# Loading w_down by whole rows and computing its two column halves together, in a two-layer mixer and mixture-of-experts kernel

## The chip, the cores and the metric

The kernel runs on one core of a Trainium2 chip. The metric is the device time of one execution in microseconds (us), the median of three runs. The core has five engines with an instruction stream each: PE (TensorE, matmuls and transposes), DVE (VectorE), ACT (ScalarE), POOL (GpSimd) and SP (SyncE, which here only issues DMAs). Each takes its instructions strictly in order, and a wait on a semaphore holds back all that is queued behind it on that engine.

## What is computed

x is 512 tokens by 1024, everything is float32. There are two layers, each a token mixer beside a cross-attention to 256 memory tokens, an output projection, a layer norm, sixteen experts of which each token uses two, and another layer norm:

```python
for i in range(DEPTH):                                  # 2 layers
    if i % 2 == 0:
        z = x @ w_in_a                                  # u | v | q
        uv = gelu(z[..., :1024]);  u, v = split(uv)
        tok = u * (W_s @ layer_norm(v, sgu_ln_g, sgu_ln_b) + sgu_b)
    else:
        z = x @ w_in_b;  tok = short_conv_mixer(...)    # uses conv_w
    xa = memory_cross_attention(q, mem, w_kv[i])
    x = layer_norm(ALPHA * x + concat(tok, xa) @ w_out[i], ln1)
    for e in range(16):                                 # chosen tokens only
        h = silu(xt @ w_gate[i, e]) * (xt @ w_up[i, e])
        f += combine[:, e] * (h @ w_down[i, e])
    x = layer_norm(ALPHA * x + f, ln2)
```

w_gate and w_up of an expert are 1024 by 512, w_down is 512 by 1024: 2 MB each, so 6 MB for an expert and 192 MB for both layers.

## The kernel before, in words

**Precision.** Every float32 product is made of three matmuls on rounded operands (mm3, L172 to L176): high by high, high by low, low by high. Each weight block is therefore split after it has landed: ACT copies it to a rounded `high` (L144), DVE (now and then POOL) subtracts to get `low` (L145). A matmul of line L174 or L176 needs `high`, one of L175 needs `low`.

**Storage.** SBUF is cut into 24 pages of 8 KB per partition. Every raw weight load, split and activation takes a page and gives it back (`page`, `drop`).

**The stream of weights** (class `Stream`, object W). `todo` is a list of loads of 1 MB, issued by SP in order as pages come free; `keep` is the number of pages that must be left free when a load is issued, `ahead` the number of splits made in advance, `flight` the number of loads under way. w_gate and w_up are read in two halves over k (4096 contiguous bytes at a time), w_down in two halves over its columns (2048 bytes at a time). An expert's loads in order are gate 0, up 0, gate 1, up 1, then the two halves of w_down of the expert before.

**An expert.** The up to 128 tokens that chose it are gathered (POOL, `xg`), transposed on PE (`xt`, L648) and copied into `xgt` by ACT in two halves. `xgt` exists once: the copy of its first half for the next expert has to wait until PE has used this expert's first halves of w_gate and w_up, and so on for the second. PE computes `ga` and `ua`, ACT takes silu of `ga` (L664), DVE multiplies (L665), PE transposes the product (`htr`), ACT and DVE split it into `ht` (L179, L180; it also exists once, so its new content waits for the last matmul that reads the old). `down` computes one column half after the other into accumulators `ya`, and ACT moves each out, scaled by the gate value, when it is complete (L686). The rows are then scattered to memory by POOL (L635). w_down of expert e-1 is computed behind gate and up of expert e; only the last expert stays on the chip and is added by a selection matmul (`ra`, L745 to L747), together with x, which SP reads back from memory (L728) after the last scatter.

**Order.** A scheduler decides the order of instructions on each engine when the program is built; it is static. So an edit to the loads also reorders ACT, DVE and PE.

**Mixer of layer 0** (L943 to L1000). After the keys and values, x is transposed and multiplied by w_in_a in three parts: q, then v (`vp`, gelu, statistics), then u (L979, gelu). `norm` (L426 to L437) normalises v: L434 subtracts the mean and multiplies by the gain, L437 multiplies by the reciprocal deviation and adds the bias; gain and bias are in page `sgln`, loaded on ACT's queue. `attend` transposes the attention weights (PE `pt`, split by ACT L179 and DVE L180), multiplies by the values (`xa`), and the results are split into `ch` and `cl`. `mx` is the product with W_s; the output projection is `oa`.

## Time and profile before

| | us |
|---|---|
| median of three runs | 1069.66 (1065.61 to 1069.82) |
| the profiled execution | 1064.45 |
| its span, first to last instruction | 1062.8 |
| outside the span | 1.65 |
| mixer of layer 0 | 0 to 217 |
| experts of layer 0 | 217 to 531 |
| layer norm, mixer of layer 1 | 531 to 725 |
| experts of layer 1 | 725 to 1040 |
| layer norm, output | 1040 to 1063 |

PE is the busiest engine; what is to be read is where it waits, for whom, and what that engine was doing. A row of the timeline gives the start, the duration, the engine, the line, the operation and, in brackets, how long the engine stood still before it and what it waited for. A row of the windows gives, for each engine, busy time in a stretch, then the granted PE clock as a share of full speed, the busy share of the 16 DMA engines, and their rate.

### The profile page before, as it was taken

What the parts mean: (1) busy time and instruction counts of PE and PEld (TensorE: products, weight loads), DVE (VectorE), ACT (ScalarE), POOL (GpSimd) and SP (SyncE); (2) the same over time, 40 slices, a digit from 0 to 9 for tenths busy, and PEclk for the clock granted to TensorE, in tenths of its full rate; (3) what the DMA queues carried; (4) which work ended last, traced back from release to release, by engine and by line L of the source; (5) the groups of instructions that cost most, each with busy time, mean ns of one, the idle gap of its engine ahead of it and who ended that gap; (6) DMA issues with size and microseconds to landing.
All of it is one profiled execution on the core that took longest, in us unless ns stands there. A gap on an engine that the chain in (4) does not pass through costs nothing.

```text
span 1062.8 us, 12859 instructions
## 1 busy us (share of the span) xinstructions
PE 989.5 (93%) x4815; PEld 809.4 (76%) x4816; DVE 779.6 (73%) x880; ACT 630.6 (59%) x684; POOL 177.1 (17%) x115
## 2 busy tenths in 40 slices
PE   8999999789999988999999999987899999988995
PEld 6788889668888876777678887875788888866863
DVE  4648657869898677878794656575799898768875
ACT  4536524458888667668553524234778887667762
POOL 0000014312212202001100000223053212220113
PEclk9999999979999999999999999987899999999998
DMA  9713449459999999979671424491699999999833
GB/s 327 269 41 119 156 162 319 160 195 360 358 370 371 367 349 365 336 274 321 200 280 40 159 79 152 146 401 45 210 355 362 372 361 360 347 359 336 282 68 154
DMA packets 102220, 273.31 MB, mean 257 GB/s; under 512 B 10442, under 2 KB 10966, under 8 KB 102152
## 3 DMA queue, kind: packets, MB, share of 16 engines
q1 hardware_dynamic: 89480, 242.84, 62.9%
q0 software_dynamic: 11808, 26.97, 9.2%
q10 hardware_dynamic: 864, 2.62, 0.7%
q8 instruction: 39, 0.64, 0.2%
q14 instruction: 29, 0.24, 0.1%
HBM read 262.22 MB, written 26.21 MB: 271 GB/s over the span
## 4 chain that ended last, share of the span: by engine, by line
PE 61%; DVE 8%; ACT 4%; DMA 4%; issue 2%; DVEq 0%; ACTq 0%; POOLq 0%; SPq 0%
PE ua L175 5%; PE ua L176 5%; PE ya L175 5%; PE ya L174 5%; PE ua L174 5%; PE ya L176 5%; PE ga L175 5%; PE ga L174 4%; PE ga L176 4%; DVE low L145 4%; ACT high L144 3%; PE xt L648 2%; PE za L176 2%; PE za L174 2%; PE za L175 2%; DMA raw<-in_w_up_dram 2%
## 5 line engine op out<-in xcount | busy, mean ns | idle before, releaser
L145 DVE TENSOR_TENSOR low<-raw,high 128x2048 fp32r<-128x2048 f32 x189 | 428.7, 2288 | 78.8 <-ACT high L144 73.0
L144 ACT ACTIVATE high<-raw 128x2048 fp32r<-128x2048 f32 x189 | 357.9, 1914 | 54.5 <-PE ga L175 20.1
L175 PE MATMUL ua<-low,xgt 128*128 128x512 f32 x248 | 98.6, 397 | 16.7 <-DVE low L145 16.6
L144 ACT ACTIVATE split<-raw 128x1024 fp32r<-128x1024 f32 x66 | 68.5, 1058 | 76.7 <-PE za L176 26.1
L174 PE MATMUL ya<-high,ht 128*128 128x512 f32 x256 | 103.9, 407 | 2.5 <-ACT high L144 2.5
L176 PE MATMUL ya<-high,ht 128*128 128x512 f32 x256 | 101.5, 398 | 2.5 <-DVE ht L180 2.5
L175 PE MATMUL ya<-low,ht 128*128 128x512 f32 x256 | 102.6, 401 | 0.7 <-DVE low L145 0.7
L174 PE MATMUL ga<-high,xgt 128*128 128x512 f32 x248 | 98.9, 399 | 3.0 <-ACT high L144 3.0
L175 PE MATMUL ga<-low,xgt 128*128 128x512 f32 x248 | 98.7, 398 | 2.1 <-DVE low L145 1.9
L174 PE MATMUL ua<-high,xgt 128*128 128x512 f32 x248 | 98.1, 395 | 0.2
L176 PE MATMUL ga<-high,xgt 128*128 128x512 f32 x248 | 97.6, 393 | 0.0
L176 PE MATMUL ua<-high,xgt 128*128 128x512 f32 x248 | 97.0, 391 | 0.0
L145 DVE TENSOR_TENSOR split<-raw,split 128x1024 fp32r<-128x1024 f32 x57 | 68.6, 1220 | 38.5 <-ACT split L144 37.8
L639 POOL DMA_INDIRECT xg<-x1d,idxs x32 | 50.3, 1572 | 248.7 <-PE xt L648 238.6
L175 PEld LDWEIGHTS ua<-low,xgt 128*128 128x128 f32 x248 | 46.6, 188 | 30.8 <-DVE low L145 21.6
L145 POOL TENSOR_TENSOR split<-raw,split 128x1024 fp32r<-128x1024 f32 x9 | 21.5, 2390 | 283.2 <-DVE sto L446 146.9
L174 PE MATMUL za<-xh,split 128*128 128x512 f32 x160 | 61.7, 392 | 2.0 <-ACT xh L179 2.0
L635 POOL DMA_INDIRECT rd<-h,idxs x16 | 41.4, 2589 | 127.0 <-ACT h L686 126.4
L175 PE MATMUL za<-xl,split 128*128 128x512 f32 x160 | 62.5, 391 | 0.0
L176 PE MATMUL za<-xh,split 128*128 128x512 f32 x160 | 61.5, 390 | 0.0
L174 PEld LDWEIGHTS ya<-high,ht 128*128 128x128 f32 x256 | 48.8, 191 | 14.3 <-ACT high L144 3.0
L176 PEld LDWEIGHTS ya<-high,ht 128*128 128x128 f32 x256 | 48.4, 189 | 14.6 <-DVE ht L180 3.4
(250 smaller groups left out, 1893.9 us busy)
## 6 DMA issues: line engine op xcount, KB each, us to landing
raw<-in_w_gate_dram SPq DMA_DIRECT2D x64, 1024.0 KB, 10.3
raw<-in_w_up_dram SPq DMA_DIRECT2D x64, 1024.0 KB, 10.1
raw<-in_w_down_dram SPq DMA_DIRECT2D x64, 1024.0 KB, 10.5
raw<-in_w_kv_dram SPq DMA_DIRECT2D x8, 1024.0 KB, 7.3
raw<-in_w_out_dram SPq DMA_DIRECT2D x8, 1024.0 KB, 5.1
raw<-in_w_in_b_dram SPq DMA_DIRECT2D x8, 1024.0 KB, 10.7
raw<-in_w_in_a_dram SPq DMA_DIRECT2D x6, 1024.0 KB, 5.5
x1d<-x POOLq DMA_DIRECT2D x8, 512.0 KB, 5.8
```

The lines of the kernel that those rows point to most:

```text
L144: act.activation(high, src, AF.Copy)
L145: (pool_e if self.on_pool(self.count) else vec).tensor_tensor(low, src, high, op=OP.subtract)
L174: pe.matmul(o, a[0], b[0], start=start, stop=False)
L175: pe.matmul(o, a[0], b[1], start=False, stop=False)
L176: return pe.matmul(o, a[1], b[0], start=False, stop=stop)
L635: added[e] = pool_e.indirect_dma_start(out=rd[i], out_offset=bass.IndirectOffsetOnAxis(ap=tabs[e][0], axis=0), in_=ys[e % 2], in_offset=No ...
L639: pool_e.indirect_dma_start(out=xg[:, e % 2], out_offset=None, in_=x1d[i], in_offset=bass.IndirectOffsetOnAxis(ap=tabs[e][0], axis=0), bou ...
L648: pe.transpose(t[:, k, :], xg[:, e % 2, k0:k0 + 2 * P - 1:2], ident)
```

## The change

- **w_down** of experts 0 to 14 is read by `rows`: a load is two k blocks of 128 rows by all 1024 columns, 4096 contiguous bytes a row. `down` takes the four splits one after the other and multiplies each with both column halves into two accumulators; both are moved out when the last block is done. The last expert keeps the old form.
- **Loads come in units of two**: both halves of a matrix are issued together when two pages are free beyond `keep`, so the loads of an expert are now gate 0, gate 1, up 0, up 1, then w_down. The order in which they are split (`plan`) is given apart from that. The `keep` numbers are raised by one or two. There is code for 2 MB pages, but their number N_DOUBLES is 0.
- **Small operands of mixer 0**: conv_w, sgu_w and sgu_b are loaded after the attention scores instead of at the start, and `sgln` after the u projection. The `norm` of v itself stands at the same place in the code, behind the u projection.

```diff
+        def rows(self, w):
+            ap = lambda k, n: bass.AP(tensor=w.tensor, offset=w.offset + k * D, ap=[[D, P], [P * D, n], [1, D]])
+            return self.add([ap(0, 2), ap(256, 2)], ap(0, 4))
...
+        def fetch(self, single=False):
+            u = self.todo.pop(0)
...
+                for src in u.parts:
+                    t = page("raw", [P, 4, 512])
+                    self.load(t, src)
+                    u.raw.append(t)
...
+            return len(free_pages) >= len(u.parts) + self.keep + max(0, self.ahead - len(self.ready))
...
         def down(e, evict):
+            if e < last:
+                a = [acc("ya") for _ in range(2)]
+                for k in range(4):
+                    g = W.next()
+                    for n in range(2):
+                        mm3(a[n], (ht[:, 0, k, :], ht[:, 1, k, :]), (g[:, 0, n, :], g[:, 1, n, :]), k == 0, k == 3)
+                    W.done(g)
+                for n in range(2):
+                    evict(n, a[n])
+                return
...
         for e in range(E):
-            gu(e, 0)
+            g, u = W.pairs(w_gate[i, e]), W.pairs(w_up[i, e])
+            d = W.rows(w_down[i, e - 1]) if e else None
+            W.use((g, 0), (u, 0))
             if e == E - 1:
-                dn(e - 1)
-            gu(e, 1)
+                W.use((d, 0), (d, 1))
+            W.use((g, 1), (u, 1))
...
-    sg = page("sgln", [P, 2, MW])
-    bcast_rows(sg[:, 0], sgu_ln_g[0])
-    bcast_rows(sg[:, 1], sgu_ln_b[0])
...
     drop(*xh, *xl)
-    W.keep = 5
+    W.keep = 6
+    sg = page("sgln", [P, 2, MW])
+    bcast_rows(sg[:, 0], sgu_ln_g[0])
+    bcast_rows(sg[:, 1], sgu_ln_b[0])
     for c in range(NC):
         norm(vp[:, c, :], sts[:, c, :], sg[:, 0], sg[:, 1], MW)
```

What this does to the order of instructions is shown at three places. The first is DVE in the mixer of layer 0, around the norm of v (L434 and L437 before, L470 and L473 now). Before:

```order
L434 SCALAR_TENSOR_TENSOR v_856<-v_856,mv,sgln_456 128x512
L437 SCALAR_TENSOR_TENSOR v_856<-v_856,rstd,sgln_456 128x512 x2
L431 TENSOR_SCALAR ve<-mv 128x1
L434 SCALAR_TENSOR_TENSOR v_856<-v_856,mv,sgln_456 128x512
L436 RECIPROCAL rstd<-sd 128x1
L437 SCALAR_TENSOR_TENSOR v_856<-v_856,rstd,sgln_456 128x512
L145 TENSOR_TENSOR split_948<-raw_582,split_948 128x1024
L436 RECIPROCAL rstd<-sd 128x1
L437 SCALAR_TENSOR_TENSOR v_856<-v_856,rstd,sgln_456 128x512
L180 TENSOR_TENSOR pt_1029<-pt,pt_1029 128x512 x2
```

Now, on the same engine:

```order
L229 TENSOR_TENSOR pt_1031<-pt,pt_1031 128x512 x2
L470 SCALAR_TENSOR_TENSOR v_853<-v_853,mv,sgln_984 128x512 x2
L473 SCALAR_TENSOR_TENSOR v_853<-v_853,rstd,sgln_984 128x512
L465 BN_AGGR mv<-vst 128x2
L229 TENSOR_TENSOR cl_1029<-xa,ch_1027 128x256
L473 SCALAR_TENSOR_TENSOR v_853<-v_853,rstd,sgln_984 128x512
L465 BN_AGGR mv<-vst 128x2
L229 TENSOR_TENSOR pt_1083<-pt,pt_1083 128x512
...
L473 SCALAR_TENSOR_TENSOR v_853<-v_853,rstd,sgln_984 128x512 x2
L229 TENSOR_TENSOR pt_1057<-pt,pt_1057 128x512 x2
```

The eight operations of the norm stood ahead of the first `pt` split; they now stand among the `pt` splits. On ACT, the two loads of `sgln` now follow the last gelu of u:

```order
L1025 ACTIVATE u_979<-za 128x512
L301 DMA sgln_984<-in_sgu_ln_g_dram 128x512
L301 DMA sgln_984<-in_sgu_ln_b_dram 128x512
L228 ACTIVATE ch_1027<-xa 128x256
L228 ACTIVATE pt_1083<-pt 128x512
L228 ACTIVATE ch_1028<-xa 128x256
L469 ACT_TABLE_LOAD
L469 ACTIVATE sd<-ve 128x1
```

The second place is ACT in layer 1, from the end of expert 10 to expert 11 (raw_7239, 7277 and raw_7276, 7278 are w_down of expert 9, raw_7297 and raw_7326 the first half of w_gate of expert 11; L664 and L700 are silu, L686 and L732 move `ya` out). Before:

```order
L144 ACTIVATE high_7485<-raw_7239 128x2048
L664 ACTIVATE h_5891<-ga 128x512
L144 ACTIVATE high_7503<-raw_7277 128x2048
L179 ACTIVATE xgt_5892<-xt 128x512
L144 ACTIVATE high_7521<-raw_7297 128x2048
L686 ACTIVATE y_170<-ya,gates 128x512
L179 ACTIVATE ht<-htr 128x512
L686 ACTIVATE y_170<-ya,gates 128x512
L144 ACTIVATE high_7559<-raw_7328 128x2048
```

Now:

```order
L700 ACTIVATE h_5887<-ga 128x512
L228 ACTIVATE xgt_5888<-xt 128x512
L179 ACTIVATE high_7485<-raw_7276 128x2048
L228 ACTIVATE xgt_5888<-xt 128x512
L179 ACTIVATE high_7501<-raw_7278 128x2048
L179 ACTIVATE high_7521<-raw_7326 128x2048
L732 ACTIVATE y_167<-ya,gates 128x512
L228 ACTIVATE ht<-htr 128x512
L732 ACTIVATE y_167<-ya,gates 128x512
L179 ACTIVATE high_7578<-raw_7328 128x2048
```

Both splits of w_down of expert 9 now stand behind a copy of `xgt`, the first one too. The block behind the evictions (raw_7328) was the first half of w_up and is the second half of w_gate now.

The third place is the last expert of layer 1 on ACT. raw_7934 and 7952 (before) and raw_8004 and 8006 (now) are w_down of expert 14, raw_7987 and raw_8007 (before) the second halves of w_gate and w_up of expert 15, raw_8038 and 8056 w_down of expert 15; the rows `h<-ya,gates` move expert 14's result out for its scatter. Before:

```order
L144 ACTIVATE high_8137<-raw_7934 128x2048
L144 ACTIVATE high_8166<-raw_7952 128x2048
L144 ACTIVATE high_8182<-raw_7987 128x2048
L144 ACTIVATE high_8199<-raw_8007 128x2048
L686 ACTIVATE h_5891<-ya,gates 128x512 x2
L144 ACTIVATE high_8217<-raw_8038 128x2048
L664 ACTIVATE h_5891<-ga 128x512
L144 ACTIVATE high_8237<-raw_8056 128x2048
```

Now:

```order
L700 ACTIVATE h_5887<-ga 128x512
L179 ACTIVATE high_8136<-raw_8004 128x2048
L179 ACTIVATE high_8166<-raw_8006 128x2048
L179 ACTIVATE high_8216<-raw_8038 128x2048
L179 ACTIVATE high_8237<-raw_8056 128x2048
L732 ACTIVATE h_5887<-ya,gates 128x512
L228 ACTIVATE ht<-htr 128x512
L732 ACTIVATE h_5887<-ya,gates 128x512
```

Expert 14's result is moved out behind all splits and the silu of the last expert, where it stood ahead of them. PE has the same order: it computes w_down of expert 14 after the whole of gate and up of expert 15, and used to compute it between their halves.

## Rows read from the trace of the kernel before

**Rows 1.** The page: busy time by engine; DMA share in 40 slices.

```profile
PE 989.5 (93%) x4815; PEld 809.4 (76%) x4816; DVE 779.6 (73%) x880; ACT 630.6 (59%) x684; POOL 177.1 (17%) x115
...
DMA  9713449459999999979671424491699999999833
```

**Rows 2.** The page: DMA issues of one matrix: KB each, median us to landing.

```profile
PE ua L175 5%; PE ua L176 5%; PE ya L175 5%; PE ya L174 5%; PE ua L174 5%; PE ya L176 5%; PE ga L175 5%; PE ga L174 4%; PE ga L176 4%; DVE low L145 4%; ACT high L144 3%; PE xt L648 2%; PE za L176 2%; PE za L174 2%; PE za L175 2%; DMA raw<-in_w_up_dram 2%
```

**Rows 3.** Busy time by stretch: us, PE, PEld, DVE, ACT, POOL, PEclk, DMA share, GB/s.

```profile
298.00:316.00 18.00, 18.00 (x86) 14.95 (x85) 16.11 (x11) 14.60 (x12) 3.96 (x2) 1.00 1.03 377
414.00:432.00 18.00, 15.94 (x73) 12.32 (x73) 14.21 (x9) 13.12 (x11) 2.63 (x2) 1.00 1.01 349
```

**Rows 4.** DMA queue in 18:36, then 414:432: packets, MB, share; then load issue, split.

```profile
q1 hardware_dynamic: 3225, 6.38, 97.0%
...
q1 hardware_dynamic: 1949, 5.55, 83.1%
...
387.14 0.37 SPq L123 DMA_DIRECT2D raw<-in_w_up_dram  x1
...
421.17 5.52 ACT L144 ACTIVATE high<-raw 128x2048 fp32r<-128x2048 f32 x3
```

**Rows 5.** Mixer 0, timeline of DVE, ACT, PE; then DMA issues: KB, us to landing.

```profile
92.93 0.74 DVE L434 SCALAR_TENSOR_TENSOR v<-v,mv,sgln 128x512 f32<-128x512 f32 x1
...
119.19 0.69 DVE L180 TENSOR_TENSOR pt<-pt,pt 128x512 fp32r<-128x512 f32 x1
119.89 0.42 DVE L180 TENSOR_TENSOR cl<-xa,ch 128x256 fp32r<-128x256 f32 x1
...
115.43 0.60 ACT L979 ACTIVATE u<-za 128x512 f32<-128x512 f32 x1
...
126.18 0.47 PE L174 MATMUL oa<-split,ch 128*128 128x512 f32 x1
...
sgln<-in_sgu_ln_g_dram ACTq DMA_DIRECT2D x1, 256.0 KB, 6.5
...
out_dram<-x SPq DMA_DIRECT2D x1, 256.0 KB, 2.0
```

**Rows 6.** Busy time by stretch, as Rows 3, at the start of layer 1's experts.

```profile
740.00:745.50 5.50, 3.27 (x15) 2.28 (x13) 3.92 (x4) 5.24 (x5) 1.29 (x1) 1.00 0.12 31
745.50:752.00 6.50, 5.76 (x17) 4.66 (x18) 5.78 (x5) 3.46 (x4) 0.00 (x0) 0.50 0.00 0
```

**Rows 7.** Timeline of ACT, DVE and PE at experts 10 and 11 of layer 0.

```profile
420.60 0.68 ACT L686 ACTIVATE y<-ya,gates 128x512 f32<-128x512 f32 x1
...
433.58 0.60 ACT L179 ACTIVATE xgt<-xt 128x512 fp32r<-128x512 f32 x1 [1.89 <-PE ua L175]
...
423.12 6.70 DVE L145 TENSOR_TENSOR low<-raw,high 128x2048 fp32r<-128x2048 f32 x3 [1.69 <-ACT high L144]
...
425.46 0.50 PE L175 MATMUL ua<-low,xgt 128*128 128x512 f32 x1 [1.83 <-DVE low L145]
```

**Rows 8.** Timeline of ACT and PE at the start of layer 1's experts.

```profile
742.50 1.28 ACT L664 ACT_TABLE_LOAD   x1
...
746.24 0.80 PE L174 MATMUL ga<-high,xgt 128*128 128x512 f32 x1 [2.98 <-ACT high L144]
```

**Rows 9.** The end: timeline of ACT, POOL, PE; then DMA issues, us to landing.

```profile
1025.27 0.69 ACT L686 ACTIVATE h<-ya,gates 128x512 f32<-128x512 f32 x1 [1.88 <-PE ya L176]
...
1026.23 1.88 POOL L635 DMA_INDIRECT rd<-h,idxs  x1 [11.97 <-ACT h L686]
...
1039.33 0.40 PE L176 MATMUL ya<-high,ht 128*128 128x512 f32 x1
1039.57 1.02 PE L745 MATMUL ra<-x,ident 128*128 128x512 f32 x2
...
rd<-h,idxs POOLq DMA_INDIRECT x1, 6.6
...
x<-rd SPq DMA_DIRECT2D x1, 512.0 KB, 5.6
```

More of the change, by code (lines that the diff above doesn't have):

```diff
@@ L62, in trunk @@
     uid = [0]
+    free_doubles = list(range(N_DOUBLES))
     def page(name, shape, dtype=FT):
@@ L128, in fetch @@
                                   reason="few loads in flight")
-            self.raw.append([t, 0])
+        def fetch(self, single=False):
+            self.sent += 1
+            u = self.todo.pop(0)
+            if u.whole is not None and free_doubles and not single:
+                u.at, t = double()
+                self.load(t, u.whole)
+                u.raw = [t[:, 0:4], t[:, 4:8]]
+            else:
+                for src in u.parts:
+                    t = page("raw", [P, 4, 512])
+                    self.load(t, src)
+                    u.raw.append(t)
+            u.left = len(u.parts)
         def split(self):
-            t, h = self.raw[0]
+            u, i = self.plan[0]
+            t, h = u.raw[i], self.half
             if self.whole and not h:
@@ L146, in split, with room @@
             self.count += 1
-            if self.raw[0][1] == 2:
-                self.raw.pop(0)
-                drop(t)
+            if self.half == 2:
+                self.half = 0
+                self.plan.pop(0)
+                u.left -= 1
+                if u.at is None:
+                    drop(t)
+                elif not u.left:
+                    free_doubles.append(u.at)
+        def room(self):
+            if not self.todo or len(self.todo) <= self.stop:
+                return False
+            u = self.todo[0]
+            if u.whole is not None and free_doubles:
+                return True
+            return len(free_pages) >= len(u.parts) + self.keep + max(0, self.ahead - len(self.ready))
         def pump(self):
             while True:
-                size = 2 if self.whole and self.raw and not self.raw[0][1] else 1
-                if not self.hold and len(self.ready) + size <= self.ahead and self.raw and len(free_pages) >= size:
+                size = 2 if self.whole and not self.half else 1
+                if (not self.hold and len(self.ready) + size <= self.ahead and self.plan and self.plan[0][0].raw
+                        and len(free_pages) >= size):
                     self.split()
-                elif len(self.todo) > self.stop and len(free_pages) > self.keep + max(0, self.ahead - len(self.ready)):
+                elif self.room():
                     self.fetch()
@@ L936, in trunk @@
     stop += len(W.todo) + W.sent
-    W.keep = 8
+    W.keep = 10
     W.after = last_mem.ins
@@ L948, in trunk @@
             keep_warm(4)
[L949 to L951 removed]
+    W.keep = 6
+    a = project_t(xh, xl)
+    qh, ql = page("qh", [P, H, S], FR), page("ql", [P, H, S], FR)
+    for h in range(H):
+        split_to(qh[:, h, :], ql[:, h, :], a[h])
+    pr = softmax_scores(qh, ql, kt)
+    drop(qh, ql, kt)
+    sgu = page("sgu", [P, 4, H, P])
+    sgw, sgb, sgt, cwr = sgu[:, 0], sgu[:, 1], sgu[:, 2], sgu[:12, 3, 0]
+    late_dma(cwr, conv_w.rearrange("o t (b p) -> (o t b) p", p=P))
+    cw = consts.tile([P, 3, 4], FT, name="cw")
+    late_dma(sgw, bass.AP(tensor=sgu_w.tensor, offset=sgu_w.offset, ap=[[P, P], [P * P, H], [1, P]]))
+    late_dma(sgb.rearrange("p h i -> p (h i)"),
+                  bass.AP(tensor=sgu_b.tensor, offset=sgu_b.offset, ap=[[0, P], [1, H * P]]))
     t = bank([P, 12], "cwt")
@@ L960, in trunk @@
     vec.memset(sgt[64:P, :, 0:64], 0.0)
-    W.keep = 4
-    a = project_t(xh, xl)
-    qh, ql = page("qh", [P, H, S], FR), page("ql", [P, H, S], FR)
-    for h in range(H):
-        split_to(qh[:, h, :], ql[:, h, :], a[h])
-    pr = softmax_scores(qh, ql, kt)
-    drop(qh, ql, kt)
     W.keep = 3
@@ L999, in trunk @@
     lnp = ln_params(ln1_g[0], ln1_b[0])
-    W.keep = 3
+    W.keep = 5
     def mixer_end(i, ch, cl, lnp):
@@ L1007, in after @@
                 W.on_pool = (lambda n: n % 2 == 1) if i == 0 else (lambda n: n % 3 != 0)
-                W.keep, W.ahead = (2, 3) if i == 0 else (1, 2)
+                W.keep, W.ahead = (3, 3) if i == 0 else (2, 2)
                 W.pump()
@@ L1079, in trunk @@
     lnp = ln_params(ln1_g[1], ln1_b[1])
-    W.keep = 3
+    W.keep = 5
     mixer_end(1, ch, cl, lnp)
```

83 lines of the change are left out of this document (40 added, 43 removed).

## The prediction

> **What bounds the kernel now.** The reader should first see in the page that PE is busy for 989.5 of 1062.8 us and that the next engine, DVE, is at 73% [rows 1]. So there are about 73 us to be won or lost around PE, and everything else shows only where PE waits. The DMA share is 9 tenths or more for most of the time in both expert stages [rows 1], and the chain of waits names loads here and there, which invites the reading that loads are the limit. The second view speaks against that: in 298:316, at DMA share 1.03, PE is busy 18.00 of 18.00 us [rows 3]. In 414:432 it loses 2.06 us, at 1.01 [rows 3], and there the load in question was issued at 387.14 and its split began at 421.17 or later, 34 us afterwards [rows 4]. A load of the experts lands some 10 us after its issue [rows 2], so it had long been there. What PE waits for in that stretch is a split: ACT moves `ya` out at 420.60, only then splits at 421.17, DVE's `low` follows at 423.12, and PE's second matmul on that block starts at 425.46 after 1.83 us of idling [rows 7]. So the early experts are bound by PE, the later ones by the order on ACT, and the bytes are hidden.
>
> **What the change does to the loads.** Longer rows save DMA time. In 18:36 only rows of 2048 bytes are loaded: 97.0% of 16 engines for 18 us and 6.38 MB is 43.8 ns per kB for one engine. In 414:432 two of five loads have such rows and three have 4096 bytes: 83.1% and 5.55 MB give 43.1 [rows 4]. With two fifths at 43.8, the long rows come to 42.6, so 1.2 ns per kB are saved on the 62.9 MB of thirty w_down matrices, 4.7 us of 16 engines. Since PE doesn't wait for these bytes I count **0**; uncovered it would be -4.7.
> The Trainium skill's page "Perfetto Trace Analysis", section "DMA Optimizations", says that going from 2 KB to 4 KB can dramatically improve throughput, where a kernel is DMA-bound. By that rule the change would be a clear gain; this trace disagrees, as 2.7% per byte is what the rows above show. "DMA: Bandwidth & Descriptors" of the Trainium skill, section "Why small descriptors are slow", has a fixed cost of 3 cycles a packet against 32 bytes a cycle; that is an estimated 2% between the two sizes, and the trace agrees with that.
>
> **The norm of v (mixer 0).** Before, `sgln` was there early, and the eight operations of the norm ran from 92.93 on, 0.74 us each, beside a busy PE [rows 5]. Now ACT issues the load only behind the last gelu of u, which ended at 116.03 (115.43 and 0.60) [rows 5]. Its landing is not in the trace at this place: 256 KB took 6.5 us in a busy queue and 2.0 in an idle one [rows 5]; DMA is nearly idle here, yet two loads follow each other and each fetches one row 128 times, so I take the middle, 4.1: about 120.2 (118.1 to 122.6). On DVE the first norm operation waits for that, and the `pt` and `cl` subtractions that PE needs are queued behind it. From 120.2 the row is eight norm operations (5.9), two `pt` (0.69 each), two `cl` (0.42 each) [rows 5] and small ones of about 0.5 between them, 8.5 us in all: 128.7. Only then are the pages free that ACT's next `pt` copies need, since one of them is `sgln`'s. Two heads remain; for each, two ACT copies, two subtractions of 0.69, six `xa` matmuls and two pairs of `ch` and `cl`, one after the other for want of work beside them, about 4 us a head: the output projection starts at 136.8, not 126.18 [rows 5]. **+10.6** (8.5 to 13.0). PE stands almost still for 10 us. At the start of layer 1's experts such a lull (3.27 of 5.50 us busy) was followed by a stretch at granted clock 0.50, the lower level, where PE worked 5.76 us [rows 6]; half of that was lost, 2.9. Here much of what follows still waits for DVE: **+1.5** (0 to 4).
> The three small loads and five transposes that leave the start: the first weights come a few us earlier, and then wait for copies of x that ACT makes anyway; now their page is written after the q projection, one projection before PE wants it. **0** (-2 to 2).
>
> **Experts, layer 0.** In experts 9 to 13 before, each lost 2.1 us as in rows 3, partly behind the evictions, and partly because the second split of w_down stood behind the copy of `xgt`, which waits for the last `ua` (433.58, after 1.89 us of idling) [rows 7]. Now the second split stands between the two copies: 0.7 saved in each of five experts. Expert 9 also lost about 1.7 on a second up block, now gone: -5.2 together. The other wait stays: `ht` and an eviction still stand ahead of the split that PE needs next, now the second gate block, at the same 0.68 + 1.84 + 2.2 [rows 4, 7]; that both evictions come at the end adds nothing, as `ht` waits for the end in either form. And experts 14 and 15, whose splits stood ahead of `ht`, now stand behind it, +1.6 and +1.8. **-1.8** (-4 to 0).
>
> **Layer 1's start.** PE idled 2.98 us at 746.24 for a gate split that stood behind silu and its table load at 742.50 [rows 8], and then ran at 0.50 [rows 6]. Now that split stands ahead of silu. At best 2.98 + 2.9; **-3** (-6 to 0).
>
> **Experts, layer 1.** Here the new order is worse: in experts 11 and 13 the first split of w_down, too, stands behind the first copy of `xgt`, which waits for the first up block. From there 0.6 + 1.84 + 2.2 us pass until `low` is there [rows 4, 7], and PE has only the second up block, 12 matmuls at 0.24 [rows 9], to cover them: 1.7 lost, plus 0.7 on the second split, in two experts: +4.8. Expert 14 loses 1.6 as above, and expert 11's second wait for an up block, about 2, goes: I take **+4** (0 to 6).
>
> **The end of layer 1.** Before, expert 14's result was moved out by 1025.96, the scatter began at 1026.23 and landed 6.6 us later, x came 5.6 after that, near 1038.6; PE finished the last expert at 1039.57 and went on with `ra` at once [rows 9]. So that chain had 1 us to spare. Now w_down of expert 14 is computed last but one. From its end, call it D, PE needs a wait for `ht` (about 2) and 24 matmuls at 0.23, so D + 7.6. The other chain needs an eviction, `ht` and an eviction, 1.5, then 6.6 + 0.1 + 5.6: D + 13.8. `ra` starts 6.2 later than PE could: **+6.1** (3 to 7). In layer 0 the same chain has several us more to spare, and I count 0.
>
> **The sum**: 10.6 + 1.5 - 1.8 - 3 + 4 + 6.1 = **+17.4**. Against the profiled execution (span and 1.65 outside it) that is 1081.9, against the median 1087.1; the profile is the fastest of four executions, whose mean is 1067.4, so I predict 1085. The ends of the terms add up to +1.5 - 2 and +30 + 2.
>
> **The rivals.**
> A. *DMA-bound after all.* For it: the full share, and the loads that the chain names [rows 1]. Against: 34 us between issue and split, 10 to landing [rows 2, 4]. Then -4.7, and the reordered splits matter less, as everything waits for bytes: 1063, faster. Chance 0.08.
> B. *Smaller stalls.* `sgln` lands in 2 us, DVE catches up sooner, and at the end the scatter or the reading back is quicker than in [rows 9]: half of the two large terms, +8 in all minus the clock's 1.5: about 1073, no change to be measured. Chance 0.13.
> C. *The added waits are hidden.* One mechanism: the static order is kept by each engine, but a wait costs only if PE has nothing queued; should the norm's operations and the last reads be early enough, only -1.8 and -3 remain: 1063, faster. It decides at a landing of `sgln` before about 117.8, when DVE finishes its first `pt` subtractions, and at 1 us of spare time at the end. Chance 0.09.
> D. *Late loads.* A pair needs two free pages beyond a larger `keep`, so it is issued up to one split cycle (5 us) later. It decides where the lead, 34 us at the example [rows 4], falls under the landing time. If in ten to fifteen late experts PE lost 1 us each, the time would be near 1098. Chance 0.12.
> The forecast itself has 0.58.
>
> **Range and chances.** A measurement tells from no change what exceeds about 0.5%, so faster is under 1064.3, slower over 1075.0. Faster: A and C, 0.17. Same: B, 0.13. Slower: 0.70. A range from 1066 to 1099 leaves out A, C and a little of D.
>
> **What would show it.** In the profile after: DVE idle at the first norm operation for the landing of `sgln`, near 116 to 120, and `oa` starting near 137 with a stretch at 0.50 around it; in layer 0 PE idling some 1.8 us per late expert on the second gate block, not the first up block; in layer 1 PE idling 2 us on the first block of w_down in experts 11 and 13; and at the end PE idle about 6 us ahead of `ra`, with the scatter of expert 14 beginning after the last split. The forecast is wrong if `oa` starts before 130, if `ra` follows the last `ya` at once, or if SP's loads land after ACT wants them.

## The result, and the profile after

The changed kernel takes 1094.66 us (median of four executions, 1093.39 to 1096.68) against 1069.53 us (1065.61 to 1069.82): a ratio of 1.0252, interval 1.0229 to 1.0275. It is slower by 2.5%. The prediction was 1085, with a range of 1066 to 1099: the side and the range were right, the centre 10 us too low.

The page of the kernel after, in its parts on engines, queues and DMA issues (KB each, median us to landing):

```profile
PE 1006.9 (92%) x4815; PEld 821.3 (75%) x4816; DVE 776.0 (71%) x880; ACT 629.4 (57%) x686; POOL 176.4 (16%) x115
...
q1 hardware_dynamic: 74120, 242.84, 59.9%
...
raw<-in_w_gate_dram SPq DMA_DIRECT2D x64, 1024.0 KB, 8.5
...
raw<-in_w_down_dram SPq DMA_DIRECT2D x64, 1024.0 KB, 8.3
```

[rows 2] shows shares of the chain of waits and not these times; the lines of before are:

```profile
raw<-in_w_gate_dram SPq DMA_DIRECT2D x64, 1024.0 KB, 10.3
...
raw<-in_w_down_dram SPq DMA_DIRECT2D x64, 1024.0 KB, 10.5
```

The same 242.84 MB go through SP's queue in fewer packets (89480 before), and a load lands about 2 us sooner. The loads are better, and the kernel is slower. PE executes the same 4815 instructions as in [rows 1] but is busy 17.4 us longer: the same matmuls take longer. That is the first sign of the clock, which the rows of the stages then show.

The profiled execution of after took 1096.68 us (span 1095.0), that of before 1064.45 (span 1062.8), so 32.2 us are to be placed. That is 7 us more than the 25.1 between the medians: this execution of after is the longest of its four, and that of before is shorter than any that was timed beside it. The table cuts the span at PE's landmarks (first `oa`, first `ga`, last `ya`, last `ra` and so on). "Clock" is worked out from both traces: PE's busy time in the stretches whose granted clock was 0.50, halved; "rest" is what remains, so the waits. It is the most that the clock can have cost, since a matmul that is slow while PE's next work waits for another engine anyway costs nothing. Before there were 5 such stretches and 13.7 us lost in them, after 15 and 31.7 us (in each kernel the last one, at the end, holds no matmul).

| stage | predicted | measured | of it clock | rest |
|---|---|---|---|---|
| to the first `oa` of layer 0 (126.18, now 138.31) | +12.1 | +12.1 | +4.9 | +7.2 |
| to the first `ga` (219.81, now 234.10) | 0 | +2.2 | +1.6 | +0.6 |
| experts of layer 0 (to 532.14, now 544.29) | -1.8 | -2.1 | +3.1 | -5.3 |
| `ra` of layer 0 (to 544.60, now 560.95) | 0 | +4.2 | +1.7 | +2.5 |
| mixer of layer 1 (to 731.55, now 755.46) | 0 | +7.6 | +4.7 | +2.9 |
| start of layer 1's experts (to the eviction of expert 4: 841.63, now 858.74) | -3 | -6.8 | -2.9 | -3.9 |
| experts of layer 1 (to 1039.33, now 1063.19) | +4 | +6.7 | +3.4 | +3.3 |
| from the last `ya` to the end | +6.1 | +8.4 | +1.4 | +7.0 |
| sum | +17.4 | +32.2 | +18.0 | +14.2 |

Without its 1.5 for the clock the prediction had 15.9, and the chip gave 14.2. For the clock the two executions give up to 18. If the rest is the same in every execution, which isn't shown, the 25.1 between the medians leave some 11 for it.

**The norm of v.** DVE, then ACT, then PE, in the timeline of after (start, us, engine, line, operation, idle before):

```profile
118.56 1.41 DVE L470 SCALAR_TENSOR_TENSOR v<-v,mv,sgln 128x512 f32<-128x512 f32 x2 [1.46 <-DMA sgln<-in_sgu_ln_g_dram]
...
124.88 1.40 DVE L473 SCALAR_TENSOR_TENSOR v<-v,rstd,sgln 128x512 f32<-128x512 f32 x2
126.94 0.69 DVE L229 TENSOR_TENSOR pt<-pt,pt 128x512 fp32r<-128x512 f32 x1 [0.66 <-ACT pt L228]
...
115.38 0.38 ACTq L301 DMA_DIRECT2D sgln<-in_sgu_ln_g_dram  x1
...
122.42 1.12 PE L447 MATMUL pt<-ident,p 128*128 128x128 f32 x4 [3.54 <-DVE ve L467]
...
127.98 0.63 PE L224 MATMUL xa<-pt,vt 128*128 128x512 f32 x1
...
138.31 0.47 PE L223 MATMUL oa<-split,ch 128*128 128x512 f32 x1
```

The load of the gain is issued at 115.38 and DVE waits for it until 118.56, 3.2 us later: earlier than the 120.2 of the prediction. From there it goes on without a pause until the last operation of the norm ends at 126.28. PE stands still for 3.54 us, later for 1.41, 0.90 and 0.96, 6.8 us in all. But `xa` matmuls now take 0.63 us and start every 0.43, where a PE at full clock starts one every 0.23. The same place in the windows (us, PE, PEld, DVE, ACT, POOL, PEclk, DMA share, GB/s):

```profile
116.00:122.00 6.00, 2.65 (x14) 1.77 (x14) 4.54 (x10) 2.65 (x6) 0.00 (x0) 0.91 0.25 87
122.00:138.00 16.00, 12.31 (x59) 9.85 (x60) 11.40 (x25) 6.27 (x16) 0.00 (x0) 0.71 0.34 114
```

Of the 16 us from 122 on, 12.31 are busy, at a mean clock of 0.71. The total of this stage was forecast to a tenth, by errors that cancel. Of its 4.9 us of clock 1.7 lie near 40 us, far ahead of the norm, and 1.5 us were won by the end of the u projection, whose first `pt` behind it starts at 115.18 instead of 114.94. From there to the first `oa` it is 23.1 us instead of 11.2, so 11.9 more: at most 3.2 of clock (1.5 was forecast) and some 8.7 of waits (10.6).

**The late experts.** PE in expert 9 of layer 0 of after:

```profile
394.66 0.40 PE L223 MATMUL ga<-high,xgt 128*128 128x512 f32 x1
396.83 0.50 PE L224 MATMUL ga<-low,xgt 128*128 128x512 f32 x1 [1.78 <-DVE low L180]
397.17 0.41 PE L225 MATMUL ga<-high,xgt 128*128 128x512 f32 x1
397.41 0.60 PE L223 MATMUL ga<-high,xgt 128*128 128x512 f32 x1
397.81 0.63 PE L224 MATMUL ga<-low,xgt 128*128 128x512 f32 x1
```

The wait is where the prediction put it, on the second gate block, with its size: 1.78 us here, and 1.79, 1.82, 1.79 and 1.81 in the next four experts. What was not foreseen begins at 397.41. The windows of the idle stretch, of what follows it and of the time after:

```profile
393.90:397.30 3.40, 1.62 (x7) 1.01 (x7) 2.81 (x2) 3.40 (x3) 1.55 (x1) 1.00 0.90 341
397.40:400.80 3.40, 3.40 (x10) 2.61 (x9) 3.40 (x2) 0.65 (x1) 0.00 (x0) 0.50 0.64 124
400.90:404.30 3.40, 3.40 (x17) 2.80 (x16) 0.85 (x2) 2.61 (x3) 0.00 (x0) 1.00 0.99 375
```

In 3.4 us at granted clock 0.50 (the lower level, 1.2 GHz) PE gets through 10 matmuls, and through 17 at full clock (2.4 GHz): about 1.7 us lost, as much as in the wait itself. Such a stretch follows three of the seven idles of 1.2 us or more in layer 0's late experts (at 397.4, 458.9 and 520.3) and two of seven in layer 1's (977.7 and 1039.1); the idles of 1.8 us that end at 418.46, 438.53 and 480.20 have none behind them. Nor had the one of before, of [rows 7]; the windows of before, up to that wait's end and behind it:

```profile
420.00:425.40 5.40, 3.56 (x15) 2.21 (x13) 3.46 (x4) 5.30 (x5) 1.60 (x1) 1.00 1.09 360
425.40:428.80 3.40, 3.34 (x15) 2.74 (x16) 3.40 (x3) 1.94 (x3) 0.00 (x0) 1.00 0.98 289
```

In layer 1 PE also waits twice on the first block of w_down, as the prediction had it, a little shorter than the 1.7 that were worked out:

```profile
943.33 0.50 PE L224 MATMUL ya<-low,ht 128*128 128x512 f32 x1 [1.46 <-DVE low L180]
...
987.98 0.50 PE L224 MATMUL ya<-low,ht 128*128 128x512 f32 x1 [1.45 <-DVE low L180]
```

**The ends of the layers.** PE and POOL in the timeline of after, then the DMA issues of 1057 to 1067 (us to landing):

```profile
546.95 1.47 PE L791 MATMUL ra<-x,ident 128*128 128x512 f32 x2 [2.27 <-DMA x<-rd]
...
1063.19 0.40 PE L225 MATMUL ya<-high,ht 128*128 128x512 f32 x1
1070.43 2.07 PE L791 MATMUL ra<-x,ident 128*128 128x512 f32 x2 [6.84 <-DMA x<-rd]
...
1058.27 1.56 POOL L671 DMA_INDIRECT rd<-h,idxs  x1 [22.45 <-DVE ht L229]
...
x<-rd SPq DMA_DIRECT2D x4, 512.0 KB, 7.5
...
rd<-h,idxs POOLq DMA_INDIRECT x1, 6.2
```

In layer 1 `ra` waits 6.84 us for x, which is read back behind the scatter that begins at 1058.27; 6.1 was forecast. In layer 0, where "several us" of spare time were counted, `ra` waits too, 2.27 us.

### The profile page after: what moved, and what is told of

Its sections match the earlier page's. It is cut to its first block, busy times and chain, and to the rows that moved or that the text cites. A ratio compares the mean times of both kernels' runs of the same rounds, so it can differ in the third digit from the quotient of the medians.

```text
span 1095.0 us, 12805 instructions
## 1 busy us (share of the span) xinstructions
PE 1006.9 (92%) x4815; PEld 821.3 (75%) x4816; DVE 776.0 (71%) x880; ACT 629.4 (57%) x686; POOL 176.4 (16%) x115
## 3 DMA queue, kind: packets, MB, share of 16 engines
q1 hardware_dynamic: 74120, 242.84, 59.9%
## 4 chain that ended last, share of the span: by engine, by line
PE 31%; issue 29%; DMA 9%; POOL 4%; DVE 3%; ACT 1%; POOLq 0%; DVEq 0%; another core or an unknown queue 0%; SPq 0%; ACTq 0%
DMA rd<-h,idxs 4%; DMA rd<-y,idxs 3%; POOL rd L671 3%; PE za L225 2%; PE za L223 2%; PE za L224 2%; PE ga L223 2%; PE ga L224 2%; PE ga L225 2%; PE ua L225 2%; PE ua L223 2%; PE ua L224 2%; POOL xg L675 2%; PE ya L225 2%; PE ya L224 2%
## 5 line engine op out<-in xcount | busy, mean ns | idle before, releaser
L224 PE MATMUL ga<-low,xgt 128*128 128x512 f32 x248 | 100.9, 407 | 16.3 <-DVE low L180 16.3
L225 PE MATMUL ya<-high,ht 128*128 128x512 f32 x256 | 101.3, 397 | 0.5 <-DVE ht L229 0.5
L223 PE MATMUL ga<-high,xgt 128*128 128x512 f32 x248 | 100.5, 405 | 0.6 <-ACT high L179 0.6
L225 PE MATMUL ga<-high,xgt 128*128 128x512 f32 x248 | 99.9, 403 | 0.0
L223 PE MATMUL ya<-high,ht 128*128 128x512 f32 x256 | 97.9, 402 | 0.6 <-ACT ht L228 0.6
L224 PEld LDWEIGHTS ga<-low,xgt 128*128 128x128 f32 x248 | 47.9, 193 | 30.4 <-DVE low L180 20.6
L224 PEld LDWEIGHTS ya<-low,ht 128*128 128x128 f32 x256 | 48.2, 188 | 15.0 <-DVE low L180 4.2
L223 PEld LDWEIGHTS ga<-high,xgt 128*128 128x128 f32 x248 | 47.9, 193 | 12.5 <-ACT high L179 1.9
```

The costliest lines, as they stand in the source:

```text
L223: pe.matmul(o, a[0], b[0], start=start, stop=False)
L224: pe.matmul(o, a[0], b[1], start=False, stop=False)
L225: return pe.matmul(o, a[1], b[0], start=False, stop=stop)
```

## The experiments

My theory after the result: the time comes from four waits that the change makes (the late `sgln`, w_down of expert 14 behind expert 15's gate and up, the splits behind the evictions, the new order in layer 1) and from the lower clock behind them. Rivals: that the two column halves computed together cost by themselves; that late loads cost; that the clock is a thing apart from the waits. Ratios are those to the kernel before, run beside each kernel.

**1. Whole rows and both halves, in the order of before.** Of the change, the kernel before gets only the new `down` and these loads; the order of loads, `keep` and the small operands stay.

```diff
+            if e < E - 1:
+                W.add_wide(w_down[i, e], 0)
+                W.add_wide(w_down[i, e], 256)
+                return
             for n in range(2):
                 W.add(w_down[i, e], 0, n * 512)
```

> The kernel before with nothing but the titled change: w_down of experts 0 to 14 in two loads of whole rows, both column halves together, block by block; order of loads, keep numbers, sgln and the small loads as before. Theory (bytes are hidden): experts up to 8 keep their period, 17.9 us. In the late experts the second split of w_down now stands ahead of the second xgt copy, which saves some 0.5 in each of eight: 1065, at most 1069. Rival A (bound by the bytes): the early experts get shorter as well, by 0.3 or more each, and the time falls by 8 or more, under 1061. Rival B (the form of down itself costs, since both evictions come together ahead of ht): some 0.7 more in each late expert, 1075.

Measured: 1066.59 us, ratio 0.9995 (0.9976 to 1.0015): no change. Its page and its window at the experts that answers to [rows 3]:

```profile
q1 hardware_dynamic: 74120, 242.84, 61.9%
...
300.00:318.00 18.00, 18.00 (x86) 14.90 (x86) 16.11 (x11) 14.69 (x13) 3.96 (x2) 1.00 1.03 373
```

The queue's time falls from 62.9% of 1062.8 us (668.5) to 61.9% of 1064.1 (658.7), so 9.8 us of 16 engines, and PE is still busy 18.00 of 18.00. The other kernels' pages give 663 to 666 us with the old rows and 653 to 660 with the new ones, so the saving is some 9 us, twice the 4.7 of the prediction. It is there and hidden; rival A is gone, and in this order the title's part of the change costs and gains nothing. "Perfetto Trace Analysis" of the Trainium skill, section "DMA Optimizations", lets one expect a large gain from 2 KB to 4 KB in a DMA-bound kernel; this kernel isn't one, by these two rows.

**2. The gain and bias of the norm.** Two kernels: after with `sgln` at the old place, before with it at the new one. The lines that the first gains:

```diff
+    sg = page("sgln", [P, 2, MW])
+    bcast_rows(sg[:, 0], sgu_ln_g[0])
+    bcast_rows(sg[:, 1], sgu_ln_b[0])
     W.keep = 6
     a = project_t(xh, xl)
```

> The changed kernel, but with sgln loaded before the q projection, where the kernel before loads it. Theory (waits set by the order): the norm of v goes back beside the u projection, the first oa matmul comes at 126 to 128 instead of 138.3, the stretch at granted clock 0.50 at 121 goes, and the time falls by 10 to 13, to about 1083. Rival 1 (loads are late since they come in units of two): oa may come earlier, but the experts take as long or longer and the time stays over 1090. Rival 2 (the clock as such): the time falls by more than 13, since fewer stretches at 0.50 occur later on as well.

> The kernel before, but with sgln loaded behind the u projection, as the changed kernel does; nothing else is changed. Theory: the first oa matmul moves from 126.2 to about 137 or 138, and the time rises by 11 to 13, to about 1081. Rival (the late norm costs only in the changed kernel, whose splits of w_out stand elsewhere): under 3, to at most 1073.

Measured: after with `sgln` early 1084.71 us, ratio 1.0143 (1.0096 to 1.0189), first `oa` at 128.94; before with `sgln` late 1077.01, ratio 1.0088 (1.0065 to 1.0112), first `oa` at 138.89, 12.7 us later than before, and about as much (12.5 to 13.0) at every landmark up to the end. The same windows as above, of after with `sgln` early:

```profile
116.00:122.00 6.00, 5.03 (x30) 3.81 (x28) 3.89 (x8) 4.50 (x10) 0.00 (x0) 1.00 0.01 3
122.00:138.00 16.00, 16.00 (x92) 13.88 (x91) 15.32 (x29) 11.03 (x21) 3.54 (x1) 1.00 0.80 282
```

From 122 on PE is busy throughout and at full clock. So the late `sgln` alone is worth about 10 us, in either kernel, and the rest of the change some 15. In after the 10 are good to some 5: the four executions with `sgln` early lie between 1076.96 and 1087.88.

Of the 2.8 us that remain at the first `oa`, 1.7 are a stretch at 0.50 near 40 us, and that one can't be put down to the change. The kernel of experiment 1 has the instructions of before, in the same order, up to its first `oa`. In both an idle of 2.00 us ends near 40 us, at 40.14 and at 40.40. The windows behind it, first of before, then of experiment 1:

```profile
40.60:43.90 3.30, 3.30 (x18) 2.24 (x17) 2.81 (x4) 1.22 (x3) 0.00 (x0) 1.00 0.90 334
...
40.60:43.90 3.30, 3.30 (x11) 2.21 (x11) 2.51 (x5) 1.29 (x2) 0.00 (x0) 0.50 0.98 367
```

The same work behind the same idle ran at full clock in one execution and at half in the other, whose first `oa` came at 128.05 instead of 126.18. About 1 us is left to the small operands, the higher `keep` and the new order.

**3. w_down of expert 14 ahead of expert 15's loads**, in after, and then the same together with `sgln` early.

```diff
+            d = W.rows(w_down[i, e - 1]) if e == E - 1 else None
             g, u = W.pairs(w_gate[i, e]), W.pairs(w_up[i, e])
-            d = W.rows(w_down[i, e - 1]) if e else None
+            if 0 < e < E - 1:
+                d = W.rows(w_down[i, e - 1])
```

> The changed kernel, but w_down of expert 14 is loaded ahead of w_gate and w_up of expert 15; on PE it then stands behind the first matmul of expert 15's up projection. Theory: the scatter of expert 14 begins some 6 us earlier against the last ya matmul, ra follows the last ya within 1 us instead of after 6.84 us of idling, and the time falls by 5 to 8, less 1 to 3 that PE then waits for ht of expert 14, so to about 1090. Rival (the end is bound by something else, the reading back or the layer norm's parameters): ra still waits 4 us or more, and the time stays at 1093 to 1095.

> The changed kernel with sgln loaded early and w_down of expert 14 loaded ahead of expert 15 (the two edits that gave back 10 and 5.5 each by itself). Theory (the two waits are separate): the gains add up, 1094.7 - 15.5, about 1079, with oa near 128 and ra within 1 us of the last ya, so 11 or 12 over the kernel before remain for the order of the loads and the clock. Rival (both give back the same clock loss): 1083 or more.

Measured: 1089.12 us, ratio 1.0215 (1.0181 to 1.0248), and with both 1078.90, ratio 1.0127 (1.0086 to 1.0167). PE at experts 14 and 15 of layer 0 of the first:

```profile
516.14 0.80 PE L223 MATMUL ga<-high,xgt 128*128 128x512 f32 x1 [4.74 <-ACT high L179]
...
545.95 0.40 PE L225 MATMUL ya<-high,ht 128*128 128x512 f32 x1
546.18 1.02 PE L791 MATMUL ra<-x,ident 128*128 128x512 f32 x2
```

`ra` follows at once, so the order of expert 14 was the cause of that wait. But ahead of expert 15's first `ga` PE now waits 4.74 us (4.75 in layer 1) for a split that stands on ACT behind two evictions and `ht`. By the stages of its trace, without the clock, the two waits of `ra` give back 8.7 us and the two expert stages take 8.2: nearly all that was won went into the new wait. The 5.5 us that the kernel is faster by go with fewer stretches at 0.50, 8 with 20.9 us lost instead of 15 with 31.7, in a trace that is one of its two shorter executions. The two edits add up (-10 and -5.5 give 1079.2), though the second kernel's executions spread from 1074.57 to 1083.63, and 1.3% are still unexplained.

**4. Both halves together, or the order of the loads?** First after with w_down read by column halves and computed half by half as before, but still in units of two:

```diff
+        def halves(self, w):
...
+            return self.add([bass.AP(tensor=w.tensor, offset=w.offset + n * 512, ap=[[D, P], [P * D, 4], [1, 512]])
+                             for n in range(2)])
...
         def down(e, evict):
-            if e < last:
-                a = [acc("ya") for _ in range(2)]
...
-            d = W.rows(w_down[i, e - 1]) if e else None
+            d = W.halves(w_down[i, e - 1]) if e else None
```

> The changed kernel, but w_down is loaded by column halves again (2048 bytes a row), still in units of two, and computed one half after the other; all else as changed. Theory (bytes are hidden, rows play no part in the loss): 1092 to 1097, the same as the changed kernel. Rival A (the rows save DMA time that is used): 1100 or more. Rival B (computing both halves together causes the loss): 1088 or less.

Measured: 1084.66 us, ratio 1.0161 (1.0138 to 1.0184). I had expected no difference from after, and it is 0.9% faster: a miss for the theory, on the side of rival B. ACT at experts 9 and 10 of this kernel, then PE:

```profile
406.82 0.69 ACT L727 ACTIVATE h<-ya,gates 128x512 f32<-128x512 f32 x1 [2.44 <-PE ya L230]
407.40 1.91 ACT L184 ACTIVATE high<-raw 128x2048 fp32r<-128x2048 f32 x1
410.36 0.60 ACT L233 ACTIVATE ht<-htr 128x512 fp32r<-128x512 f32 x1 [1.05 <-PE ya L229]
410.85 0.68 ACT L727 ACTIVATE h<-ya,gates 128x512 f32<-128x512 f32 x1
411.42 5.51 ACT L184 ACTIVATE high<-raw 128x2048 fp32r<-128x2048 f32 x3
...
411.69 0.50 PE L229 MATMUL ga<-low,xgt 128*128 128x512 f32 x1 [0.50 <-DVE low L185]
...
415.71 0.50 PE L229 MATMUL ga<-low,xgt 128*128 128x512 f32 x1 [1.01 <-DVE low L185]
```

The first half is moved out at 406.82 while the second is still computed, and a split fits in behind it. When the down projection ends, 1.06 us of `ht` and one eviction stand ahead of the next split instead of 1.64, and PE's wait is cut in two, 0.50 and 1.01 instead of 1.79. That is 0.3 us an expert directly. The two traces differ by 6.9 us, and up to 5.8 of that is clock: 10 low stretches and 25.9 us lost instead of 15 and 31.7.

Then after with whole rows and both halves together, but each load a unit of its own, in the order of before:

```diff
+            def one(u, k):
+                W.use((W.add([u.parts[k]]), 0))
             g, u = W.pairs(w_gate[i, e]), W.pairs(w_up[i, e])
             d = W.rows(w_down[i, e - 1]) if e else None
-            W.use((g, 0), (u, 0))
+            del W.todo[-(3 if e else 2):]
+            one(g, 0), one(u, 0)
             if e == E - 1:
-                W.use((d, 0), (d, 1))
-            W.use((g, 1), (u, 1))
+                one(d, 0), one(d, 1)
+            one(g, 1), one(u, 1)
             if 0 < e < E - 1:
-                W.use((d, 0), (d, 1))
+                one(d, 0), one(d, 1)
```

> The changed kernel with rows, late sgln and all other edits, but the experts' loads come one by one in the old order: gate 0, up 0, gate 1, up 1, with w_down of expert 14 between the halves of expert 15. Theory (units and their order make what the late sgln does not): oa still at 138, but from the last layer 0 ya to the end no more than 3 us are lost, ra follows ya at once in both layers, and the time is 1077 to 1081, as in the kernel before with sgln late. Rival (the raised keep numbers or the late small loads matter): 1085 or more.

Measured: 1072.72 us, ratio 1.0063 (1.0037 to 1.0089), lower than expected, and equal within the intervals to before with `sgln` late. `ra` follows `ya` at once in both layers. So the loads in units of two, with their order, cost some 20 us, twice as much as `sgln`; the units and the order were not tried apart. My terms for that order came to +5.3 (-1.8, -3, +4 and +6.1). Much of the difference can be clock: over all executions the mean granted clock is 0.9585 for after and 0.968 here, at most 10 us in 1080.

With `sgln` early as well (the diff of 2), both costs should be gone:

> The changed kernel with the experts' loads one by one in the old order and with sgln loaded early: of the change remain the whole rows, both halves together, the raised keep numbers and the late small loads. Theory (what cost time were the late norm and the units' order): the late norm's 10 are taken off the 1072.7 that the old order gave, which makes 1060 to 1064, faster than the kernel before by some 0.5%, since the copy of xgt no longer stands ahead of the second w_down split and layer 1 starts without waiting for silu. Rival (the gains of the old-order kernel hung on its later start): 1067 or more.

Measured: 1068.80 us, ratio 1.0011 (0.9996 to 1.0026). No longer slower, but a miss of several us for the theory, which had the gains in layer 1's start and the experts kept; the rival had 1067 or more. An early `sgln` is worth 3.9 us here and not 10. The first `oa` is back at 129.13, yet four stretches at 0.50 appear in the experts (430.2, 471.2, 512.1 and 942.2), behind idles of 1.3 to 1.8 us.

**5. The clock by itself.** If the low stretches follow from PE's short idles, matmuls that nobody reads should remove them. `keep_warm` is the kernel's own function for such matmuls, on a constant page into an accumulator of their own; here seven of them are put behind each down projection from expert 7's on. The edit was made in after, in the kernel of the last paragraph, and in before.

```diff
                 scatter(e - 1)
+                if e >= 8:
+                    keep_warm(7)
```

> The changed kernel with 7 matmuls on constants added behind each down from expert 8 on; the program's order puts them where PE idles for the split behind the evictions. They compute nothing that is used. Theory (the idling of 1.8 us costs twice, since some of these idles are followed by 3.4 us at granted clock 0.50): the stretches at 0.50 inside the expert stages go, 1.6 each, four or five of them, and the time falls by 4 to 8. Rival 1 (the clock falls in any case, or its fall is hidden): within 2 of the changed kernel. Rival 2 (the added matmuls delay PE): 4 or more slower.

> The kernel of e9 with 7 matmuls on constants behind each down from expert 8 on, which do nothing but keep PE busy where it idles. Theory (only clock, few falls to avoid here): no stretch at 0.50 inside the expert stages, 0 to 3 less than e9. Rival (they delay PE or push other instructions about): 3 or more above e9.

> The kernel before with the 7 idle matmuls behind each down from expert 8 on and nothing else, to see what part of e10's gain is theirs alone. Theory (the kernel before loses 1.6 us to the clock in its expert stages, the rest of e10's gain comes from the new order): 1063 to 1067. In its program the second w_down split also moves ahead of the second xgt copy, which saves some 0.5 in each of eight experts. Rival (the idle matmuls are all of it): 1060 or less, the same as e10.

Measured: after 1091.32 us, ratio 1.0230 (1.0210 to 1.0250), 3.3 less than without, a little short of what was expected; the old order with `sgln` early **1059.61** (six executions, 1058.22 to 1060.16), ratio 0.9929 (0.9912 to 0.9946), 9.2 less than without, where 0 to 3 had been expected; before 1062.19, ratio 0.9948 (0.9930 to 0.9966), between the theory's range and the rival's. The windows of the late experts of both layers, with the old order and `sgln` early, first without the added matmuls:

```profile
380.00:540.00 160.00, 143.39 (x615) 111.55 (x614) 118.45 (x78) 106.93 (x90) 22.15 (x14) 0.96 0.86 300
870.00:1035.00 165.00, 156.61 (x713) 126.42 (x713) 131.05 (x86) 118.53 (x100) 27.12 (x17) 0.99 0.84 295
```

and with them:

```profile
380.00:540.00 160.00, 156.58 (x705) 118.70 (x704) 128.76 (x96) 112.87 (x99) 22.10 (x14) 1.00 0.90 315
870.00:1035.00 165.00, 162.91 (x752) 127.25 (x751) 125.25 (x84) 111.61 (x95) 30.32 (x16) 1.00 0.84 291
```

The clock is at 1.00 in both stages, and the spans differ by 9.5 us (1067.7 and 1058.2), of which the low stretches make 8.9 (21.4 and 12.5 us lost). The clock is thus no thing apart: filling the idles brings it back. What that is worth is less clear. With the added matmuls the scheduler also orders ACT, DVE and PE otherwise from the late experts of layer 0 on, and the two effects were not tried apart. Stage by stage the clock and the time agree less well than in the sum: layer 0's experts get 10.5 us shorter with 6.9 less lost, layer 1's 1.4 longer with 1.6 less lost.

In after the low stretches of the experts go, too: 1.5 us are lost in the two expert stages instead of 10.2. But these stages get only 3.3 us shorter, since the added matmuls take 8 to 9 us of PE's time in each. The waits for `sgln` and `ra` remain, and the mixer's loss. The kernel before gains 5.3 us by the same line, so most of the best version's gain has nothing to do with the change. Of those 5.3 the clock can give at most 3.5 (its mean over all executions goes from 0.9715 to 0.9748). Between the best version and before with the added matmuls 0.2% are left, and their intervals overlap: a gain of the change is not shown.

**6. The mixer of layer 1**, where nothing was predicted and 7.6 us were lost. At the layer norm ahead of the experts POOL now takes a split. DVE and POOL in after there:

```profile
725.30 3.39 DVE L470 SCALAR_TENSOR_TENSOR x<-x,mv,ln 128x1024 f32<-128x1024 f32 x1
728.61 1.21 DVE L180 TENSOR_TENSOR split<-raw,split 128x1024 fp32r<-128x1024 f32 x1
...
725.26 2.34 POOL L180 TENSOR_TENSOR split<-raw,split 128x1024 fp32r<-128x1024 f32 x1
```

The edit keeps these splits off POOL:

```diff
-                W.on_pool = (lambda n: n % 2 == 1) if i == 0 else (lambda n: n % 3 != 0)
+                W.on_pool = (lambda n: n % 2 == 1) if i == 0 else (lambda n: False)
```

> The changed kernel, but in the layer norm of layer 1 no split is given to POOL. In the changed kernel's trace a DVE operation of that norm takes 3.39 us (x<-x,mv,ln at 725.30) while POOL subtracts (725.26 to 727.60); the like one before took 1.27. Theory (DVE is held up while POOL subtracts): the DVE operation takes 1.3 again; the splits now take 1.2 to 2.3 of DVE's own time each, so layer 1's first ga comes 0 to 3 earlier against its last oa, and the time falls by 0 to 3. Rival (the 3.39 has another cause): it stays over 2.5.

Measured: 1092.78 us, ratio 1.0241 (1.0218 to 1.0264), which the intervals don't part from after. The row itself is clear:

```profile
724.59 1.28 DVE L470 SCALAR_TENSOR_TENSOR x<-x,mv,ln 128x1024 f32<-128x1024 f32 x1
```

1.28 us instead of 3.39. But from the last `oa` to the first `ga` it is 31.71 us instead of 32.43 (29.12 before), and 0.4 of that is clock, so this explains 0.7 us at most. Of the stage's 7.6 the clock has up to 4.7; about 2 stay open.

## Why the prediction came out right, and where it was wrong

- **The loads: 0.** Right. The saving was some 9 us of DMA time instead of 4.7, so about 5% per byte of w_down instead of the 2.7% read from [rows 4] and the 2% estimated beside it, all hidden (experiment 1).
- **The norm of v: +10.6 and +1.5 of clock.** The mechanism was right, wait and order included; that the sum met the stage to a tenth (12.1) was luck. `sgln` came at 118.56 instead of 120.2 and DVE was through at 126.28 instead of 128.7. But what follows took 12.0 us up to `oa` and not two heads of "about 4 us": 18 of the 24 `xa` matmuls were still to come, where 12 had been counted. That a lull is followed by the lower clock was read from [rows 6]. PE was busy 6.4 us of a stretch of 10.2 at 0.50; of that 4.2 lie without a pause behind the last operation of the norm, so 2.1 were lost there instead of 1.5. What PE did slowly before that was hidden behind DVE's row.
- **The clock elsewhere: not counted.** This is the term that was mis-sized: 1.5, against up to 18 between the two profiled executions and some 11 between the medians. It is most of why the centre was 10 us too low. The prediction priced each wait of the late experts at its own length. On the chip five of fourteen idles of 1.2 to 1.8 us had a stretch at half clock behind them that cost up to another 1.7 each, and the same happened at both `ra` and in the mixers.
- **Layer 0's experts: -5.2 for five, +3.4 for experts 14 and 15.** Both sizes were wrong. Expert 14's `htr` comes 13.9 us later than before, expert 8's 14.1, and two low stretches (3.4 us) lie between them, so without the clock it is -3.6 for the five. From there to the last `ya` it is -1.7: an idle of 2.48 us for `ht`, at 525.59 in before, is gone. The whole stage gives -5.3 without the clock, and that it came to -2.1 in all, near the -1.8, was the clock's doing. "That both evictions come at the end adds nothing" was wrong by 0.3 us an expert, and by more through the clock (experiment 4).
- **The end of layer 0: 0.** Wrong: 2.27 us of waiting for x. The spare time was estimated, not taken from a row, though the same chain was worked out for layer 1.
- **The mixer of layer 1: not looked at.** +7.6, of which up to 4.7 is clock and at most 0.7 POOL beside DVE. The edit to the stream changed which splits fall to POOL there, which the order of the changed kernel would have shown.
- **Layer 1's start: -3 (-6 to 0).** -6.8, beyond the range: wait and low stretch at that place both went, the "at best" of the prediction, and about 1 us more. The middle was taken without a reason from a row.
- **Layer 1's experts: +4.** Right but for the clock: +3.3 without it, +6.7 with it. Both waits on w_down came, 1.46 and 1.45 us instead of 1.7.
- **The end: +6.1.** Right: 6.84 us of waiting, by the chain that was worked out. The scatter took 6.2 us instead of 6.6; the four transfers that read x back took 7.5 in the median, where one of them had been taken at 5.6.

Of the rivals, none happened. D came near in time (1098) by a wrong mechanism: loads land sooner than before, and by the waits of its trace ACT never stands still for one in the expert stages.

In sum over the experiments: `sgln` about 10 us, the loads in units of two with their order about 20 (of which expert 14's place 5 to 6), whole rows and halves computed together nothing in the old order, and near 10 in the new one, where the evictions fall on the path. These are times of whole kernels, with the clock in them; how the clock falls in a given execution, and so how much of each is its, stays open. The parts overlap: the first two undone together bring 26 us, not 30.

## What to carry to other kernels

A wait of PE is to be priced with the clock behind it: look in the trace of before for what the granted clock did after idles of that length, and count a share of them twice over. What longer DMA rows are worth was settled here by one window in which PE is fully busy at full DMA share; what the change does to the order of splits and evictions then decides. Where a static order leaves short idles on PE that can't be removed, a few matmuls that nobody reads may pay more than the change itself: here 0.5% on the kernel before and 0.9% on the mended one, but 0.3% on after, where they took nearly as much of PE's time as they gave back.

## What was not expected of the hardware

- A stretch of 3.4 us at granted clock 0.50 behind a PE idle of only 1.3 to 1.8 us, in a stage where PE is busy some 90% of the time. Behind nine of fourteen idles of that kind there was none, in the same kernel, and behind the idle of 2.00 us near 40 us one execution has the stretch and another hasn't (experiment 2). So a count of idles gives no more than bounds.
- Executions of one kernel differ by about as much as their clock: ten spans of the kernel with the old load order go from 1065.4 us at a mean granted clock of 0.974 to 1076.6 at 0.962. Part of what looks like noise of a kernel is this. With the added matmuls six spans lay between 1056.5 and 1058.4, at 0.977 to 0.978.
- A DVE operation on 128x1024 took 3.39 us instead of 1.28 while POOL subtracted for 2.34 us; it started 0.04 us after POOL and ended 1.09 us after POOL had ended. "Perfetto Trace Analysis" of the Trainium skill, section "Optimizing Scalar/DVE Operations", says that the two engines share a read port of SBUF, so that moving work between them might not help; the trace agrees.
